# A hybrid convolution and attention layer on one core: column sums, weight norms and the first squares take another place in the order

## The chip, the cores and the metric

The kernel runs on one core of one Trainium2 chip. The metric is device time in microseconds (us) of one execution; the kernel before has a median of 2218.2 us over 3 runs (2217.41 to 2220.26). Its engines are TensorE (PE in the profile, its weight loads PEld), VectorE (DVE), ScalarE (ACT), GpSimd (POOL) and SyncE (SP), which here only starts DMAs.

## The reference

One layer on 4096 tokens of width 1024, in float32:

```
h = rmsnorm(x, norm_w)
u, g_b, g_c, z_conv, q, k, v, z_attn = split(h @ w_in, 8 pieces of 512 columns)
y_conv = g_b * (conv3(g_c * u, conv_w) + conv_b) * silu(z_conv)      # depthwise, width 3
q, k = rmsnorm(q, q_norm_w), rmsnorm(k, k_norm_w)                    # per head, 8 heads of 64
o = mix over (window, dilation) in ((128,1), (512,4), (2048,16)) of
    banded attention(q, k, v, T5 bias), weighted by a softmax over their log-sum-exps
y_attn = o * silu(z_attn)
out = x + concat(y_conv, y_attn) @ w_out
```

## The kernel before

Matmuls run in float16. Each operand is multiplied by a scale factor and split in a high and a low float16 part; a product is three matmuls, high·high, high·low and low·high (L401, L402, L403), summed in one PSUM bank. There are 8 banks of 128 x 512 float32.

**First phase** (to about 740 us of the trace). The tokens are cut into 32 tiles of 128. For each tile PE multiplies the tile by four groups of 512 columns of w_in: group 4 (q), 5 (k), 6 (v) and 7 (z, the attention's gate). One group of one tile is `mm`: 8 pieces of 128 along the depth, times 3, so 24 matmuls into one bank. Tile t uses the banks b0 to b0+3 with b0 = 4·(t mod 2), in the order q, k, v, z, so two tiles in a row fill the eight banks in turn. Tiles 0 and 1 are done together at the start, while the weights are still arriving: their q go to banks 0 and 1, k to 2 and 3, v to 4 and 5, z to 6 and 7.

What follows a group: `post_qk1` (ACT squares the bank, DVE L417 sums per head, DVE L237 and POOL L238 begin the inverse root by a power), `post_qk2` (DVE L244 to L247 finish it, DVE L425 reads the bank, ACT and DVE L433 split it, POOL L435 copies for k), `post_v` (DVE L448, ACT L450, DVE L451, store L452), `post_z` (ACT tanh L456, DVE L457, POOL L458, store L459). `x_split(t + 1)` makes the next tile ready: ACT L382 and DVE L383 write its high and low part, and two DMAs from SP's queue transpose them (L385). PE can start the next tile's q when both have landed. The input rows of tile t + 3 are asked of SP's queue by `load_x` (L204).

**v_sums, v_scales, v_gate.** The scale of v's columns comes from sums of absolute values of v's weights. PE adds them with 8 matmuls against ones (L475) into bank 1, DVE L476 reads the bank, L479 and L480 make the factor `vs` that `post_v` uses, L484 and L485 the factor that `post_z` uses. `post_v` and `post_z` of tiles 0 and 1 stand behind that.

**w_scale.** Each group of weights has one scale, from its norm. The weights come in 8 pieces of 128 x 512. ACT squares a piece and sums it (`w_square`), or DVE takes a maximum instead (`w_max`, L263). When all 8 are done, DVE L271 adds them, PE multiplies the 128 x 1 column by ones in bank 7 (L273, recorded as 2 instructions), DVE L274 reads it, POOL L276 takes a power, DVE L277 and on write the scales. `w_split` (ACT L295, DVE L296) then makes the two float16 parts of each piece. At the start this is done for group 4: four calls of `square` (each a `w_square` and a `w_max`), and among them `x_parts(1)`, which splits tile 1's transposed x from PSUM (ACT L375, DVE L376).

**conv_w_tasks.** The four convolution groups of w_in (order 0, 2, 3, 1) are scaled and split for the second phase by background tasks: for each group 8 loads with squares, then 8 loads with splits. From tile 4 on, `run_tasks` puts a batch of tasks behind `post_qk1` of k and another behind `post_z`, in each tile.

**What sets the order.** The schedule is written by hand: the order of the code is the order on each engine, each engine runs its own instructions strictly in that order, and waits between engines are semaphores. The pools of buffers (`wk`, `h16` with 3 buffers each, the staging buffers) give a new tile the buffer that comes free. `bias_copies` (L511) puts one DMA of 0.6 MB into ACT's queue in each of the tiles 10 to 17.

**Second phase.** Banded attention for three dilations, the convolution's matmuls (L838 to L840) and the output projection. Its first loads read the q and k that the first phase stored last.

Of the kernel before, what the change touches and what calls it, by code (L numbers as in the profile page):

```python
# [65 lines left out]
def tile_hybrid_block(  # L66
# [39 lines left out]
    def bank(n, shape, dt=F32):  # L106
        return ps.tile(shape, dt, name=f"bank{n % 8}")
# [57 lines left out]
    def run_tasks(tasks, n=None):  # L165
        for _ in range(len(tasks) if n is None else min(n, len(tasks))):
            tasks.pop(0)()
# [95 lines left out]
        nc.vector.tensor_reduce(wss[:, cg, kt:kt + 1], src, axis=AX.X, op=OP.max, apply_absolute_value=True)  # L263

    def w_scale(cg, maxima=0):
        if maxima:
            t = wss[:, cg, KT - maxima:]
            nc.vector.tensor_tensor(t, t, nwc[:, KT - maxima:], op=OP.mult)
            nc.vector.tensor_tensor(t, t, t, op=OP.mult)
        tot = pa.tile([128, 2], F32, name="wtot", bufs=2)  # L270
        nc.vector.tensor_reduce(tot[:, 0:1], wss[:, cg], axis=AX.X, op=OP.add)  # L271
        p = bank(7, [128, 512])
        nc.tensor.matmul(p[:, 0:1], ones, tot[:, 0:1], start=True, stop=True)  # L273
        nc.vector.tensor_scalar(tot[:, 1:2], p[:, 0:1], 1e-30, None, op0=OP.max)  # L274
        s = wsc[:, cg:cg + 1]
        nc.gpsimd.tensor_tensor(s, tot[:, 1:2], mhalf[:, 0:1], op=OP.pow)  # L276
        nc.vector.tensor_scalar(s, s, W_TOP, None, op0=OP.mult)  # L277
        nc.vector.tensor_scalar(nws[:, cg], nwc, s, None, op0=OP.mult)
        i = inv[:, cg:cg + 1]
        nc.vector.reciprocal(i, s)  # L280
        nc.vector.tensor_scalar(i, i, 1.0 / H_SCALE, None, op0=OP.mult)
        if cg in (4, 5):
            mul = 1.0 if cg == 4 else QK_SCALE
            c = rqs[:, cg - 4]
            nc.vector.tensor_scalar(c[:, 1:2], i, -0.5 * mul, None, op0=OP.mult)
            nc.vector.tensor_scalar(c[:, 2:3], i, 1.5 * mul, None, op0=OP.mult)
            nc.vector.tensor_scalar(c[:, 0:1], i, i, 1.0 / DH, op0=OP.mult, op1=OP.mult)
        if cg == 1:
            nc.vector.tensor_tensor(i, i, inv[:, 3:4], op=OP.mult)
        if cg in (3, 7):  # L290
            nc.vector.tensor_scalar(cz[:, cg // 4:cg // 4 + 1], i, 0.5, None, op0=OP.mult)
# [16 lines left out]
    wc = [[[None] * 4 for _ in range(4)] for _ in range(2)]  # L308

    def conv_w_tasks():  # L310
        tasks, got = [], {}
        todo = []
        for e, j in enumerate(CJ):
            todo += [(e, j, kt, 0) for kt in range(KT)] + [(e, j, kt, 1) for kt in range(KT)]

        def dma(n):
            e, j, kt, _ = todo[n]
            got[n] = stage_in(w_in_piece(j, kt))

        def use(n):  # L320
            e, j, kt, second = todo[n]
            src = got.pop(n)
            if not second:
                w_square(j, kt, src)
                if kt == KT - 1:
                    w_scale(j)
                return
            for sweep in range(2):
                if kt % 2 == 0:
                    wc[sweep][e][kt // 2] = wpool.tile([128, 2, 2, 256], F16, name=f"w{16 * sweep + 4 * e + kt // 2}")  # L330
                w = wc[sweep][e][kt // 2][:, kt % 2]
                w_split(w[:, 0], w[:, 1], src[:, 256 * sweep:256 * sweep + 256], j, kt)

        tasks += [lambda n=n: dma(n) for n in range(3)]
        for n in range(len(todo)):
            tasks.append(lambda n=n: use(n))
            if n + 3 < len(todo):
                tasks.append(lambda n=n: dma(n + 3))
        return tasks
# [31 lines left out]
    def x_parts(t, banks):  # L371
        hi, lo = h_views(t)
        for g, p in enumerate(banks):
            s = slice(4 * g, 4 * g + 4)
            nc.scalar.activation(hi[:, s], p, AF.Copy)  # L375
            nc.vector.tensor_tensor(lo[:, s], p, hi[:, s], op=OP.subtract)  # L376
# [17 lines left out]
    def mm(ts, j, cg, between=None, run=1):  # L394
        out = [bank(j + n, [128, 512]) for n in range(len(ts))]
        for k0 in range(0, KT, run):
            for n, (p, t) in enumerate(zip(out, ts)):
                hi, lo = HT[t]
                for kt in range(k0, k0 + run):
                    w = wa[(cg - 4) * 8 + kt]  # L400
                    nc.tensor.matmul(p, hi[:, kt, :], w[:, 0], start=kt == 0, stop=False)  # L401
                    nc.tensor.matmul(p, hi[:, kt, :], w[:, 1], start=False, stop=False)  # L402
                    nc.tensor.matmul(p, lo[:, kt, :], w[:, 0], start=False, stop=kt == KT - 1)  # L403
                    if n == len(ts) - 1:
                        for task in (between or {}).get(kt, ()):
                            task()
        return out
# [37 lines left out]
    def post_v(t, p):  # L445
        v16 = pa.tile([128, H, 128], F16, name="h16", bufs=3)
        v32 = pa.tile([128, 512], F32, name="wk", bufs=3)
        nc.vector.tensor_tensor(v32, p, vs, op=OP.mult)  # L448
        pv = v32.rearrange("p (h d) -> p h d", h=H)
        nc.scalar.activation(v16[:, :, 0:DH], pv, AF.Copy)  # L450
        nc.vector.tensor_tensor(v16[:, :, DH:128], pv, v16[:, :, 0:DH], op=OP.subtract)  # L451
        nc.sync.dma_start(v_d[t * 128:(t + 1) * 128], v16)  # L452

    def post_z(t, p):
        sz = pa.tile([128, 512], F32, name="wk", bufs=3)
        nc.scalar.activation(sz, p, AF.Tanh, scale=cz[:, 1:2])  # L456
        nc.vector.scalar_tensor_tensor(sz, sz, 1.0, p, op0=OP.add, op1=OP.mult)  # L457
        nc.gpsimd.tensor_tensor(sz, sz, vinv, op=OP.mult)  # L458
        nc.sync.dma_start(sz_d[t * 128:(t + 1) * 128], sz)  # L459
# [10 lines left out]
            nc.scalar.activation(VA[n], wa[16 + n][:, 0], AF.Abs)  # L470

    def v_sums():
        pcs = bank(1, [128, 512])
        for n in range(KT):
            nc.tensor.matmul(pcs, ones16, VA[n], start=n == 0, stop=n == KT - 1)  # L475
        nc.vector.tensor_scalar(vinv, pcs, 1e-30, None, op0=OP.max)  # L476

    def v_scales():
        nc.vector.reciprocal(vs, vinv)  # L479
        nc.vector.tensor_scalar(vs, vs, V_SCALE / H_SCALE, None, op0=OP.mult)  # L480

    def v_gate():

        nc.vector.tensor_scalar(vinv, vinv, inv[:, 6:7], inv[:, 7:8], op0=OP.mult, op1=OP.mult)  # L484
        nc.vector.tensor_scalar(vinv, vinv, 0.5 * H_SCALE / (V_SCALE * P_SCALE), None, op0=OP.mult)  # L485
# [54 lines left out]
    xp1 = x_transpose(1, 6)  # L540
    for n in range(4):
        square(4, n)
        if n == 1:
            x_parts(1, xp1)
    w_scale(4, 4)

    def each(f, *a):
        return lambda: f(*a)
# [1 line left out]
    def parts(cg):  # L550
# [10 lines left out]
    pv = mm((0, 1), 4, 6, {5: [each(w_scale, 7, 4)], 7: parts(7) + [  # L561
        each(stats1, 2), gains, each(post_qk1, 0, "q", pq[0]), each(stats2, 2)]})
# [8 lines left out]
    per = -(-len(tw) // (NT - 6))  # L571
    pq = mm((2,), 0, 4)[0]
    qk_store(1, "k")
    v_sums()
    v_scales()
    post_v(0, pv[0])
    post_v(1, pv[1])
    v_gate()
    post_z(0, pz[0])
    post_z(1, pz[1])  # L580
    for t in range(2, NT):
        b0 = 4 * (t % 2)
        post_qk1(t, "q", pq)
        if t + 3 < NT:
            load_x(t + 3)
        if t + 1 < NT:
            x_split(t + 1)
        post_qk2(t, "q")
        pk = mm((t,), b0 + 1, 5)[0]
        if 6 <= t < 9:  # L590
            bias_load(t - 6)
        post_qk1(t, "k", pk)
        if t + 2 < NT:
            stats1(t + 2)
        if t > 3:
            run_tasks(tw, per // 2)
        pv = mm((t,), b0 + 2, 6)[0]
        qk_store(t, "q")
        if t % 2 and t + 1 < NT:
            h_store(t // 2)  # L600
        post_qk2(t, "k")
        if t + 2 < NT:
            stats2(t + 2)
        post_v(t, pv)
        pz = mm((t,), b0 + 3, 7)[0]
        post_z(t, pz)
        if t > 3:
            run_tasks(tw, per - per // 2)
        if t + 1 < NT:
            pq = mm((t + 1,), 4 - b0, 4)[0]  # L610
        qk_store(t, "k")
        if 6 <= t < 9:
            bias_rows(t - 6)
        if 10 <= t < 10 + H:
            bias_copies(t - 10)
        if t == 12:
            taps()
        if t == 13:
            nc.vector.tensor_scalar(cw, cw, 0.5, None, op0=OP.mult)
        if t == NT - 3:  # L620
            load_h(0)
        if t == NT - 2:
            load_h(1)
# [319 lines left out]
    for gi, (pr, g, grp) in enumerate(groups):  # L943
        d = DILS[g]
        for b in range(8):
            if d == 16:
                n, nb = b % 2, 2
                vidx = (b // 2 + 4 * n, b // 2 + 4 * (1 - n))
            elif d == 4:
                n, nb, vidx = b, 8, (b, b + 1)  # L950
            else:
                n, nb, vidx = 8 * grp + b, 32, (b, b + 1)
# [191 lines left out]
    for u in range(NU):  # L1144
# [44 lines left out]
        n = u - LAG  # L1189
# [109 lines left out]
```

## Time and profile before

| what | value |
|---|---|
| median of 3 runs | 2218.2 us (2217.41 to 2220.26) |
| the profiled execution | 2221.63 us, span of the trace 2219.8 us |
| mean granted TensorE clock | 0.987 |
| PE busy | 2112.3 us, 95% of the span |
| DVE busy | 1440.1 us, 65% |
| ACT busy | 1071.0 us, 48% |
| POOL busy | 846.4 us, 38% |

The span is the trace's own time, from its first instruction to its last; the execution's time is 1.83 us longer. Times in the rows are counted from the start of the span. The granted clock is the share of its full speed that TensorE was allowed; it stands at 1.0 or at 0.5. A time in brackets behind a row is how long the engine had been idle before, and what released it.

### The profile page before, as it was taken

The numbers are of one execution on the slowest core, as the hardware profiler recorded it, in microseconds if no ns is written. First come the engines' busy times: TensorE is split into PE (matmuls) and PEld (weight loads), VectorE is DVE, ScalarE is ACT, GpSimd is POOL, SyncE is SP. The second block draws the span as 40 slices with busy tenths as digits, with TensorE's granted clock in tenths as the row PEclk, the third lists the DMA queues.
The fourth block names the chain that finished last, engine by engine and source line by source line (L and its number), as shares of the span: only waits on it lengthen the run. The fifth ranks groups of instructions, "written<-read, shape, count | busy, mean of one in ns | idle before, by whom it ended". The sixth has DMA issues, their size and how long they took to land. (4 is left out here: it accounts for less than half of the span.)

```text
span 2219.8 us, 48689 instructions
## 1 busy us (share of the span) xinstructions
PE 2112.3 (95%) x17718; PEld 1561.8 (70%) x17718; DVE 1440.1 (65%) x4031; ACT 1071.0 (48%) x3095; POOL 846.4 (38%) x1635
## 2 busy tenths in 40 slices
PE   7799999999999989999999999999999999999999
PEld 3344444444444778888888898888888887788887
DVE  6765655656565356766666666676666666887776
ACT  5433333333332156666666666676666664222221
POOL 0332322222322255433554335543353353344332
PEclk9999999999999999999999999999999999999999
DMA  5365567875654877779755896858966567687775
GB/s 200 95 176 154 153 173 163 205 162 156 169 165 134 180 157 144 149 160 179 154 140 129 175 195 135 175 139 173 189 135 151 123 121 221 208 266 243 240 247 184
DMA packets 627118, 378.36 MB, mean 170 GB/s; under 512 B 403393, under 2 KB 569404, under 8 KB 620732
## 3 DMA queue, kind: packets, MB, share of 16 engines
q1 hardware_dynamic: 505508, 304.71, 55.5%
q10 hardware_dynamic: 121368, 70.53, 12.4%
q8 instruction: 139, 2.28, 0.4%
q14 instruction: 103, 0.84, 0.1%
HBM read 174.54 MB, written 110.39 MB: 128 GB/s over the span
## 5 line engine op out<-in xcount | busy, mean ns | idle before, releaser
L838 PE MATMUL bank<-hb,w 128*128 128x256 f16 x2048 | 562.2, 275 | 0.3 <-ACT cu L845 0.3
L839 PE MATMUL bank<-hb,w 128*128 128x256 f16 x2048 | 562.2, 274 | 0.0
L840 PE MATMUL bank<-hb,w 128*128 128x256 f16 x2048 | 562.1, 274 | 0.0
L401 PE MATMUL bank<-wa,hb 128*128 128x512 f16 x1024 | 392.0, 383 | 17.0 <-DVE vinv L476 12.1
L403 PE MATMUL bank<-wa,hb 128*128 128x512 f16 x1024 | 391.5, 382 | 5.7 <-DMA hb<-xs 5.7
L402 PE MATMUL bank<-wa,hb 128*128 128x512 f16 x1024 | 391.8, 383 | 0.3 <-DVE wa L296 0.2
L1042 DVE CUSTOM_DVE_ANT_0 L<-bank,bt,alpha 128x256 f32<-128x256 f32 (+1 forms) x768 | 318.7, 452 | 111.9 <-PE bank L1030 81.6
L1051 ACT ACTIVATE L<-L,ot 128x256 f32<-128x256 f32 (+1 forms) x768 | 363.5, 476 | 27.9 <-DVE ot L1042 21.7
L1003 POOL COPY qz<-qk 64x128 f16<-64x128 f16 x512 | 156.4, 305 | 166.6 <-PE bank L1030 149.0
L840 PEld LDWEIGHTS <-w 128*128 128x128 f16 x2048 | 201.8, 99 | 24.6
L839 PEld LDWEIGHTS <-w 128*128 128x128 f16 x2048 | 201.8, 99 | 23.3 <-issue 0.5
L238 POOL TENSOR_TENSOR rs_rq<-rs_mq,mhalf 128x8 f32<-128x8 f32 x64 | 110.9, 1732 | 278.2 <-DVE rs_mq L237 275.8
L838 PEld LDWEIGHTS <-w 128*128 128x128 f16 x2048 | 201.9, 99 | 20.6
L1086 DVE SCALAR_TENSOR_TENSOR pt<-bank,pt 128x512 f16<-128x512 f32 x192 | 132.6, 690 | 119.0 <-ACT pt L1074 118.3
L1074 ACT ACTIVATE pt<-bank 128x512 f16<-128x512 f32 x192 | 114.6, 597 | 174.6 <-PE bank L1068 168.4
L402 PEld LDWEIGHTS <-hb 128*128 128x128 f16 x1024 | 100.9, 99 | 135.4 <-issue 18.1
L1105 PE MATMUL bank<-vt,pt 128*128 128x64 f16 x1536 | 176.6, 194 | 20.4 <-DMA pt<-src 16.5
L1090 DVE SCALAR_TENSOR_TENSOR src<-L,src 128x384 f16<-128x384 f32 (+1 forms) x192 | 131.6, 685 | 96.9 <-ACT src L1080 89.9
L403 PEld LDWEIGHTS <-hb 128*128 128x128 f16 x1024 | 100.9, 98 | 132.6 <-DMA hb<-xs 9.2
L401 PEld LDWEIGHTS <-hb 128*128 128x128 f16 x1024 | 101.7, 99 | 127.6 <-issue 6.2
L1107 PE MATMUL bank<-vt,pt 128*128 128x64 f16 x1536 | 176.9, 194 | 0.0
L1106 PE MATMUL bank<-vt,pt 128*128 128x64 f16 x1536 | 176.8, 194 | 0.0
(200 smaller groups left out, 4472.8 us busy)
## 6 DMA issues: line engine op xcount, KB each, us to landing
hb<-hT SPq DMA_DIRECT2D x32, 1024.0 KB, 6.9
o_d<-ot ACTq DMA_DIRECT2D x32, 528.0 KB, 5.1
qk<-o_d SPq DMA_DIRECT2D x63, 264.0 KB, 3.7
hT<-hb SPq DMA_DIRECT2D x16, 1024.0 KB, 4.1
wst<-in_w_in_dram SPq DMA_DIRECT2D x64, 256.0 KB, 2.9
qk<-in_x_dram SPq DMA_DIRECT2D x32, 512.0 KB
qk_d<-h SPq DMA_DIRECT2D x128, 96.0 KB, 3.4
vt<-v_d ACTq DMA_DIRECT2D x48, 256.0 KB, 4.5
```

The source lines that it names most:

```text
L401: nc.tensor.matmul(p, hi[:, kt, :], w[:, 0], start=kt == 0, stop=False)
L402: nc.tensor.matmul(p, hi[:, kt, :], w[:, 1], start=False, stop=False)
L403: nc.tensor.matmul(p, lo[:, kt, :], w[:, 0], start=False, stop=kt == KT - 1)
L838: nc.tensor.matmul(pt, w_h, hi[:, :, kt], start=kt == 0, stop=False)
L839: nc.tensor.matmul(pt, w_h, lo[:, :, kt], start=False, stop=False)
L840: nc.tensor.matmul(pt, w_l, hi[:, :, kt], start=False, stop=kt == KT - 1)
L1003: nc.gpsimd.tensor_copy(QZ[u % QZB][i][half], cols(q_t[i], U["qc"], half))
L1042: nc.vector.tensor_tensor_reduce(out=L[:, i], in0=p[i][:, 0:kn], in1=bias[:, U["b0"]:U["b0"] + kn], scale=alpha, scalar=BIG, op0=OP.add, o ...
L1051: nc.scalar.activation(L[:, i], L[:, i], AF.Exp, scale=-1.0, bias=ot[:, b, i, DH:DH + 1], accum_out=ot[:, b, i, DH + 1:DH + 2])
L1105: nc.tensor.matmul(p[:, i], hi, v[:, 0:DH], start=j == 0, stop=False)
L1106: nc.tensor.matmul(p[:, i], hi, v[:, DH:], start=False, stop=False)
L1107: nc.tensor.matmul(p[:, i], lo, v[:, 0:DH], start=False, stop=j == 1)
```

## The change

Three edits, all of the order of work; nothing is computed in another way.

First, `w_scale` becomes a generator `w_scale_steps` that pauses once, between DVE's sum (L271) and PE's matmul (L273). At the start all four `square` of group 4 are issued, then DVE's sum, then `x_parts(1)`, then the rest of the scale. Second, for the convolution's groups the part up to the pause stays where it was, behind the last square, and the rest is issued by the first task that splits a piece of that group. Third, `v_sums`, `v_scales`, `post_v` and `post_z` of tiles 0 and 1 are gathered in `late()`, which is called in tile 2 behind the k group's matmuls; the sums go to bank 3 instead of bank 1.

```diff
+    def w_scale_steps(cg, maxima=0):
         ...
         nc.vector.tensor_reduce(tot[:, 0:1], wss[:, cg], axis=AX.X, op=OP.add)
+        yield
         p = bank(7, [128, 512])
         nc.tensor.matmul(p[:, 0:1], ones, tot[:, 0:1], start=True, stop=True)
...
                 if kt == KT - 1:
-                    w_scale(j)
+                    scale.append(w_scale_steps(j))
+                    next(scale[0])
                 return
+            if kt == 0:
+                for _ in scale.pop():
+                    pass
             for sweep in range(2):
...
     def v_sums():
-        pcs = bank(1, [128, 512])
+        pcs = bank(3, [128, 512])
...
     for n in range(4):
         square(4, n)
-        if n == 1:
-            x_parts(1, xp1)
-    w_scale(4, 4)
+    scale = w_scale_steps(4, 4)
+    next(scale)
+    x_parts(1, xp1)
+    run_tasks([lambda: list(scale)])
...
     pq = mm((2,), 0, 4)[0]
     qk_store(1, "k")
-    v_sums()
-    v_scales()
-    post_v(0, pv[0])
-    post_v(1, pv[1])
-    v_gate()
-    post_z(0, pz[0])
-    post_z(1, pz[1])
+    def late():
+        v_sums()
+        ...
+        post_z(1, pz[1])
     for t in range(2, NT):
...
         pk = mm((t,), b0 + 1, 5)[0]
+        if t == 2:
+            late()
```

In the rows of the order, the line numbers of the changed kernel are 4 to 9 higher for the same instruction.

On VectorE at the start, before the first projection; `w_158` to `w_164` are the staged pieces of group 4, `hb_261` is the low part of tile 1's x. Before:

```order
L263 TENSOR_REDUCE wss<-w_158 128x1
L263 TENSOR_REDUCE wss<-w_160 128x1
L376 TENSOR_TENSOR hb_261<-bank_272,hb_261 128x512
L376 TENSOR_TENSOR hb_261<-bank_277,hb_261 128x512
L263 TENSOR_REDUCE wss<-w_162 128x1
L263 TENSOR_REDUCE wss<-w_164 128x1
L268 TENSOR_TENSOR wss<-wss,nwc 128x4
L269 TENSOR_TENSOR wss<-wss 128x4
L271 TENSOR_REDUCE wtot<-wss 128x1
L274 TENSOR_SCALAR wtot<-bank_302 128x1
```

and of the change:

```order
L263 TENSOR_REDUCE wss<-w_158 128x1
L263 TENSOR_REDUCE wss<-w_160 128x1
L263 TENSOR_REDUCE wss<-w_162 128x1
L263 TENSOR_REDUCE wss<-w_164 128x1
L272 TENSOR_TENSOR wss<-wss,nwc 128x4
L273 TENSOR_TENSOR wss<-wss 128x4
L275 TENSOR_REDUCE wtot<-wss 128x1
L385 TENSOR_TENSOR hb_261<-bank_272,hb_261 128x512
L385 TENSOR_TENSOR hb_261<-bank_277,hb_261 128x512
L279 TENSOR_SCALAR wtot<-bank_302 128x1
```

The two subtractions of `x_parts(1)` moved from among the four maxima to behind the sum.

On TensorE at the end of tile 2's q, the last two of the eight sums and what follows them; `wa_117` is the first piece of k's weights, `wa_125` of v's. Before:

```order
L475 LDWEIGHTS ones_220
L475 MATMUL bank_829<-w_696,ones_220 128x512
L475 LDWEIGHTS ones_220
L475 MATMUL bank_829<-w_698,ones_220 128x512
L401 LDWEIGHTS hb_646
L401 MATMUL bank_891<-wa_117,hb_646 128x512
```

and of the change:

```order
L484 LDWEIGHTS ones_220
L484 MATMUL bank_880<-w_696,ones_220 128x512
L484 LDWEIGHTS ones_220
L484 MATMUL bank_880<-w_698,ones_220 128x512
L410 LDWEIGHTS hb_646
L410 MATMUL bank_931<-wa_125,hb_646 128x512
```

The sums now stand behind tile 2's 24 matmuls of k and ahead of those of v, instead of ahead of k's.

On VectorE in the same place, behind the last instruction of tile 1's k (L433, L442 of the change). Before:

```order
L433 TENSOR_TENSOR h_795<-wk,h_795 128x4x128
L476 TENSOR_SCALAR vinv<-bank_829 128x512
L479 RECIPROCAL vs<-vinv 128x512
L480 TENSOR_SCALAR vs<-vs 128x512
L448 TENSOR_TENSOR wk<-bank_524,vs 128x512
L451 TENSOR_TENSOR h_841<-wk,h_841 128x8x64
L448 TENSOR_TENSOR wk<-bank_525,vs 128x512
L451 TENSOR_TENSOR h_847<-wk,h_847 128x8x64
L484 TENSOR_SCALAR vinv<-vinv,inv 128x512
L485 TENSOR_SCALAR vinv<-vinv 128x512
L457 SCALAR_TENSOR_TENSOR wk<-wk,bank_634 128x512
L457 SCALAR_TENSOR_TENSOR wk<-wk,bank_635 128x512
```

and of the change:

```order
L442 TENSOR_TENSOR h_795<-wk,h_795 128x4x128
L426 TENSOR_REDUCE ssq<-wk 128x8
L237 TENSOR_SCALAR rs_mq<-ssq,rqs 128x8
L392 SCALAR_TENSOR_TENSOR xs_839<-xt,rs_rx,xs_838 128x1024
L244 TENSOR_TENSOR rs_t_844<-rs_rq 128x8
L245 TENSOR_TENSOR rs_t_844<-rs_t_844,rs_mq 128x8
L246 TENSOR_SCALAR rs_t_844<-rs_t_844,rqs 128x8
L247 TENSOR_TENSOR rs_rq<-rs_rq,rs_t_844 128x8
L434 TENSOR_TENSOR wk<-bank_800,rs_rq 128x512
L437 TENSOR_TENSOR wk<-wk,cvec 128x512
L442 TENSOR_TENSOR h_852<-wk,h_852 128x4x128
L485 TENSOR_SCALAR vinv<-bank_880 128x512
```

The work of tile 2's q and the split of tile 3 went ahead of the eleven instructions on v and z of tiles 0 and 1; before, they stood right behind them.

## Rows read from the trace of the kernel before

**Rows 1.** The page, part 1: busy us (share of the span) x instructions.

```profile
PE 2112.3 (95%) x17718; PEld 1561.8 (70%) x17718; DVE 1440.1 (65%) x4031; ACT 1071.0 (48%) x3095; POOL 846.4 (38%) x1635
```

**Rows 2.** PE's waits, whole span: waited for; us, times, longest.

```profile
PE bank L1105 <- DMA pt<-src: 16.5, 6, 5.7
PE bank L273 <- DVE wtot L271: 13.2, 5, 3.9
PE bank L401 <- DVE vinv L476: 12.1, 1, 12.1
```

**Rows 3.** Timeline of PE, start: start us, us, engine line op.

```profile
20.79 0.58 PE L401 MATMUL bank<-wa,hb 128*128 128x512 f16 x1 [2.09 <-ACT wa L295]
```

**Rows 4.** Timeline of DVE, start.

```profile
12.69 1.27 DVE L263 TENSOR_REDUCE wss<-w 128x1 f32<-128x512 f32 x2
...
15.46 0.69 DVE L376 TENSOR_TENSOR hb<-bank,hb 128x512 f16<-128x512 f32 x1 [0.16 <-ACT hb L375]
16.07 1.27 DVE L263 TENSOR_REDUCE wss<-w 128x1 f32<-128x512 f32 x2
...
17.84 0.16 DVE L271 TENSOR_REDUCE wtot<-wss 128x1 f32<-128x8 f32 x1
18.74 0.16 DVE L274 TENSOR_SCALAR wtot<-bank 128x1 f32<-128x1 f32 x1 [0.74 <-PE bank L273]
```

**Rows 5.** Timeline of PE, tiles 2 to 4.

```profile
74.81 1.90 PE L475 MATMUL bank<-w,ones 128*128 128x512 f16 x8
88.76 0.59 PE L401 MATMUL bank<-wa,hb 128*128 128x512 f16 x1 [12.05 <-DVE vinv L476]
...
107.62 0.39 PE L403 MATMUL bank<-wa,hb 128*128 128x512 f16 x1 [0.22 <-DMA hb<-xs]
...
127.92 0.38 PE L401 MATMUL bank<-wa,hb 128*128 128x512 f16 x1
```

**Rows 6.** Timeline of DVE, tiles 2 and 3.

```profile
86.03 0.69 DVE L425 TENSOR_TENSOR wk<-bank,rs_rq 128x512 f32<-128x512 f32 x1
...
98.74 0.68 DVE L417 TENSOR_REDUCE ssq<-wk 128x8 f32<-128x512 f32 x1
...
99.59 2.30 DVE L383 SCALAR_TENSOR_TENSOR xs<-xt,rs_rx,xs 128x1024 f16<-128x1024 f32 x1
...
107.12 0.68 DVE L417 TENSOR_REDUCE ssq<-wk 128x8 f32<-128x512 f32 x1
...
117.81 1.27 DVE L383 SCALAR_TENSOR_TENSOR xs<-hb,rs_rx,xs 128x1024 f16<-128x1024 f32 x1
```

**Rows 7.** Timeline of POOL, tile 2.

```profile
98.31 2.51 POOL L458 TENSOR_TENSOR wk<-wk,vinv 128x512 f32<-128x512 f32 x2 [9.73 <-DVE wk L457]
```

**Rows 8.** Timeline of SP's queue, the transposes for tiles 3 and 4.

```profile
102.16 3.35 SPq L385 DMA_TRANSPOSE hb<-xs  x2
...
121.51 4.21 SPq L385 DMA_TRANSPOSE hb<-xs  x2
```

**Rows 9.** Timeline of PE, line 273, the convolution's second to fourth scale.

```profile
346.41 0.38 PE L273 MATMUL bank<-wtot,ones 128*128 128x1 f32 x2 [2.52 <-DVE wtot L271]
491.54 0.58 PE L273 MATMUL bank<-wtot,ones 128*128 128x1 f32 x2 [3.86 <-DVE wtot L271]
629.83 0.38 PE L273 MATMUL bank<-wtot,ones 128*128 128x1 f32 x2 [1.67 <-DVE wtot L271]
```

**Rows 10.** Windows of 5 us: PE, PEld, DVE, ACT, POOL busy, granted clock, DMA share, GB/s.

```profile
346.50:351.50 5.00, 5.00 (x17) 2.05 (x18) 0.93 (x6) 0.00 (x0) 0.80 (x2) 0.66 0.81 293
491.50:496.50 5.00, 4.96 (x17) 2.24 (x18) 2.42 (x12) 0.63 (x1) 1.80 (x4) 0.68 0.14 42
497.00:502.00 5.00, 5.00 (x25) 2.29 (x24) 2.42 (x7) 0.63 (x1) 0.55 (x1) 1.00 0.06 22
```

**Rows 11.** SP's queue near tile 15: timeline, then waits of 345 to 370 us.

```profile
356.65 10.80 SPq L385 DMA_TRANSPOSE hb<-xs  x2
...
SPq L385 <- DMA bv_d<-vec_d: 7.7, 1, 7.7
```

More of the change, by code (lines that the diff above doesn't have):

```diff
@@ L265, in w_scale @@
     def w_scale(cg, maxima=0):
+        for _ in w_scale_steps(cg, maxima):
+            pass
+    def w_scale_steps(cg, maxima=0):
         if maxima:
@@ L310, in conv_w_tasks @@
     def conv_w_tasks():
-        tasks, got = [], {}
+        tasks, got, scale = [], {}, []
         todo = []
@@ L325, in use @@
                 if kt == KT - 1:
-                    w_scale(j)
+                    scale.append(w_scale_steps(j))
+                    next(scale[0])
                 return
+            if kt == 0:
+                for _ in scale.pop():
+                    pass
             for sweep in range(2):
@@ L573, in tile_hybrid_block @@
     qk_store(1, "k")
-    v_sums()
-    v_scales()
-    post_v(0, pv[0])
-    post_v(1, pv[1])
-    v_gate()
-    post_z(0, pz[0])
-    post_z(1, pz[1])
+    def late():
+        v_sums()
+        v_scales()
+        post_v(0, pv[0])
+        post_v(1, pv[1])
+        v_gate()
+        post_z(0, pz[0])
+        post_z(1, pz[1])
     for t in range(2, NT):
```

## The prediction

> **What bounds the kernel now.** I read the page's part 1 first: PE is busy 95% of the span and no other engine over 65% [rows 1], so only time in which PE stands still, or runs at the lower clock, can be won. Next I read PE's waits [rows 2]. The change names three of them: 12.1 us before the first matmul of tile 2's k, once, until DVE L476 has read the column sums; 13.2 us in five waits for DVE's sum ahead of a scale (L273), of which three of the convolution's four are moved (2.52, 3.86 and 1.67 us) [rows 9]; and the start, where the first projection matmul comes at 20.79 us [rows 3]. Then I read the timelines of PE, DVE, POOL and SP around each place, to see what would hold PE back next. Two sizes serve everywhere. PE's step from matmul to matmul is (127.92 − 107.62) / 94 = 0.216 us [rows 5], so a group of 24 takes 5.2 us and a tile of 96 takes 20.7. And an idle stretch on PE is dear beyond its length: behind the wait of 3.86 us a window of 5 us holds 17 matmuls at a granted clock of 0.68, a later one 25 at 1.00 [rows 10], so the lower clock adds about 8 x 0.216 = 1.7 us. The waits of 12.05 and 3.86 us are followed at once by matmuls of 0.59 us instead of 0.38 [rows 5, 9]; the wait of 1.67 is not.
>
> **The start.** The scale of group 4 is a chain: four maxima on DVE, the sum L271, PE L273, DVE L274, POOL's power, the first split, PE's first L401 at 20.79 [rows 3, 4]. Between the second and third maximum stand tile 1's two L376 and a wait for ACT. In the new order the third maximum can start at 12.69 + 1.27 = 13.96 instead of 16.07, 2.1 us earlier, and the sum ends at 18.00 − 2.1 = 15.9. PE's matmul and its way back to L274 take 18.74 − 18.00 = 0.74, but the two L376 now lie in just that gap (0.69 and about 0.6): L274 waits for them, to about 17.2 instead of 18.74. I take −1.5 us; the bounds are −2.1 (if DVE's queue did not matter) and 0 (if the split waits for something else, such as the pieces' arrival).
>
> **Tile 2.** Before, PE ends the sums at 76.7 and stands idle until DVE L476 releases bank 1 at 88.76, because DVE works through q and k of tiles 0 and 1 first. Now PE goes on from 74.81 with tile 2's k, to 80.0. The sums follow, but in bank 3, which tile 1's k holds until DVE's L425 of 86.03 has ended at 86.72 [rows 6]: so 6.7 of the 12.05 us stay as idle time, only later. Sums at the lower clock to about 90.2, v to 95.4. Then z needs bank 3 too, and with it L476, which now stands behind tile 2's q and the split of tile 3 (about 8 us of DVE) and comes at about 95.5: no further wait to speak of. z and tile 3's q end at about 106.6, against 112.4 before: PE is up to 5.8 us ahead, and with 72 matmuls more would reach tile 4 at 122.1, where it stood there at 127.92.
>
> What is late next is tile 4's x. Its transposes leave SP at 121.51 to 125.72 behind L383 of 117.81 [rows 6, 8]; tile 3's left SP at 105.51 and were used by the first L403 that waited for them at 107.62 [rows 5, 8], 2.1 later, so tile 4's landed at about 127.8. That chain is DVE's, from 86.03 on, one instruction behind the other: the v and z work of tiles 0 and 1 (88 to 98.8), tile 2's q (L417 of 98.74), tile 3's split, tile 2's k (L417 of 107.12), tile 4's split (117.81). The change exchanges the first with the next two and leaves nothing out. Two of its members change: L383 of 99.59 took 2.30 us beside POOL's L458 against 1.27 for the other [rows 6, 7], which may now save 1.0; and k's power on POOL now queues behind the two L458 of 1.25 each [rows 7], which may cost 1.0. Queued behind it on DVE are k's remaining steps and L383 of tile 4, and behind that SP. So x lands at about 127.8 again, PE stands idle about 5 us before tile 4 and starts it at 127.5 (its high part needs only the first transpose), 0.4 us earlier, and behind a wait of that length comes the lower clock, +1.7. Before, the 12 us were followed by the same low stretch, which I have counted in the 90.2. I take **+1.3**. The bounds: −5.8 if DVE's chain holds PE nowhere, and +2.4 if the two z stores, which share the buffers of `wk`, also hold up tile 2's k.
>
> **The convolution's scales.** The first scale stays where it was, because its sum and its first split fall in the same batch: there the change does nothing. The second to fourth matmul moves two groups (48 matmuls, 10.4 us) later, long behind its sum, so the waits of 2.52, 3.86 and 1.67 us go [rows 9].
>
> - Second (346.41): 2.52 and a low stretch (17 matmuls, 0.66 [rows 10]), together 4.2 us at that place. But tile 15's x is late already: the second transpose stands in SP's queue for 7.7 us behind a copy of the biases and leaves only at 367.45 [rows 11], so it lands at about 369.5 by the 2.1 above. PE reached tile 15 at 346.66 + 96 x 0.216 + 1.7 + 0.4 (small waits) = 369.5 and did not wait. Four us earlier it waits four, and pays for the lower clock after it: 0 to +1.7, I take **+0.8** (bounds −4.3 and +1.7).
> - Third (491.54): 3.86 and its low stretch of 1.7. No copies of biases are left there and the transposes land well ahead: **−5.5** (−4.2 to −5.8).
> - Fourth (629.83): 1.67, no low clock behind it: **−1.8** (0 to −2).
>
> What hides the moved DVE and POOL work is that PE has 48 matmuls between; if that cover is gone (third rival) the splits come late.
>
> **Sum.** −1.5 + 1.3 + 0.8 − 5.5 − 1.8 = −6.7: from the profiled execution's 2221.6 (span 2219.8 and 1.8 around it) to 2214.9. That execution lies 3.4 above the median, so the forecast is 2218.2 − 6.7 = **2211.5 us**.
>
> **Rivals.** (1) *The transposes do not hold PE back.* At tile 15 alone the sum becomes −6.7 − 0.8 − 4.3 = −11.8, 2206.4; at tile 4 as well −11.8 − 1.3 − 5.8 = −18.9, 2199.3. For it: both landings are inferred from one tile's. Against it: the 7.7 us are a row of SP's own waits. The Trainium skill, "DMA: Bandwidth & Descriptors", section "Issuing engines are not separate DMA queues", says that DMAs started by different engines run on the same 16 DMA engines and interleave; by that rule a transpose would share the engines with the copy rather than stand behind it. The row shows it standing behind the copy, so the trace does not bear the rule out at this place. Chances 0.10 and 0.07.
>
> (2) *The gain is swallowed at the second phase.* PE there waits six times for DMAs of `pt`, 16.5 us in all, the longest 5.7 [rows 2]. If those transfers are bound by data that start with the phase and not with PE, up to 5.7 come back: 2217.2. Against it: their loads follow the last stores of the first phase, which move with PE. Chance 0.15.
>
> (3) *Slower.* The scale now stands right in front of its own splits. ACT's and DVE's splits wait for POOL's power, which can stand behind another power in the middle of a tile; the staging buffers come free later, SP's loads for them wait, and the next tile's transposes are behind those in SP's queue. It decides when the transposes of tiles 21 and 28 land more than 5.5 and 1.8 us behind where PE would then be. With each landing 3.3 us behind PE's arrival of before: −1.5 + 1.3 + 0.8 + 2 x 3.3 = +7.2, 2225.4. Against it: SP has no such wait elsewhere except behind the copies. Chance 0.05.
>
> **How the numbers follow.** The forecast has 0.60 and the rivals 0.10, 0.07, 0.15 and 0.05; 0.03 is left for low stretches that come or go elsewhere. A difference of 0.2%, 4.4 us, is about what a measurement of this kernel can tell from none. The forecast's own bounds are 2207 to 2215.5, since tile 4, tile 15 and the scales each carry about 1.7 us of clock. The range reaches over most of (1) and (2): 2204 to 2217.5. Faster: three quarters of the forecast, all of (1) and some of (2), 0.71. Same: the rest of both, 0.23. Slower: 0.06.
>
> **What would show it.** Right: the first L401 at about 19.3; PE's wait at the sums now for L425 and near 6.7 us; a wait of about 5 us for `hb` before tile 4 and of about 4 before tile 15; PE's waits for L271 down from 13.2 to about 5; tiles from 21 on 5 to 7 us earlier than before. Wrong: tile 4 starts near 122, or `hb` is waited for at tiles 21 and 28, or the last L403 of the first phase comes earlier and the end does not.

## The result, and the profile after

The changed kernel took 2205.0 us (median of 4 runs, 2200.2 to 2209.6), the kernel before beside it 2217.8: a ratio of 0.9943, 95% interval 0.9918 to 0.9969. Timed again beside the experiments it took 2208.7 (12 runs, 2203.8 to 2216.3) against 2216.5 (35 runs): 0.9970, 0.9954 to 0.9985. By these ratios the gain is 12.6 us in the first set and 6.6 in the second, which has three times the runs; the forecast was 6.7. The two intervals overlap between 7 and 10 us. The profiled execution took 2209.58 us with a span of 2207.8.

PE's busy time fell by 2.2 us and the span by 12.0: most of the gain is time in which PE stood idle.

```profile
PE 2110.1 (96%) x17718; PEld 1559.2 (71%) x17718; DVE 1436.5 (65%) x4031; ACT 1071.7 (49%) x3095; POOL 846.7 (38%) x1635
```

PE's waits over the whole span of the change (waited for: us in total, times, longest), against [rows 2]:

```profile
PE bank L1120 <- DMA pt<-src: 11.3, 5, 4.6
...
PE bank L410 <- DMA hb<-xs: 7.9, 4, 4.4
PE bank L484 <- DVE wk L434: 6.6, 1, 6.6
PE bank L412 <- DMA hb<-xs: 6.4, 8, 1.5
...
PE bank L278 <- DVE hb L385: 2.3, 1, 2.3
...
PE bank L410 <- ACT w L300: 2.0, 1, 2.0
PE bank L278 <- DVE wtot L275: 1.8, 1, 1.8
```

The 12.1 us for L476 are gone and 6.6 us for L434 (L425 before) stand in their place; of the 13.2 us for the scales' sums one wait of 1.8 is left, the first of the convolution's four, and group 4's 3.4 us have become 2.3 us for L385; the waits of the first matmul of a tile for its x (`hb`) have grown, 7.9 us where there had been 1.4. PE's timeline at the places that answer to [rows 3, 5] and to the second scale of [rows 9]:

```profile
17.10 0.59 PE L278 MATMUL bank<-wtot,ones 128*128 128x1 f32 x2 [2.26 <-DVE hb L385]
19.77 0.59 PE L410 MATMUL bank<-wa,hb 128*128 128x512 f16 x1 [2.08 <-ACT wa L300]
...
85.26 3.59 PE L484 MATMUL bank<-w,ones 128*128 128x512 f16 x8 [6.62 <-DVE wk L434]
...
125.05 0.61 PE L410 MATMUL bank<-wa,hb 128*128 128x512 f16 x1 [4.37 <-DMA hb<-xs]
...
344.37 0.39 PE L410 MATMUL bank<-wa,hb 128*128 128x512 f16 x1 [1.72 <-DMA hb<-xs]
...
390.38 0.39 PE L410 MATMUL bank<-wa,hb 128*128 128x512 f16 x1 [2.00 <-ACT w L300]
...
726.40 0.38 PE L412 MATMUL bank<-wa,hb 128*128 128x512 f16 x1
```

The bracket at 390.38 names ACT's split of a convolution weight, which this matmul does not read. With the scales alone (below) the same wait is put down to `hb`, and in both PE goes on 1.2 us after SP is done with tile 16's transposes, so I take it for a wait for `hb`.

The last row is the last matmul of the first phase. Before, it stood here, followed by the second phase's first:

```profile
733.46 0.38 PE L403 MATMUL bank<-wa,hb 128*128 128x512 f16 x1
733.67 0.27 PE L838 MATMUL bank<-hb,w 128*128 128x256 f16 x1
```

So the first phase gives 733.46 − 726.40 = 7.1 us, and the second phase of this one pair of traces 4.9 more. The same group in the two traces, at the groups where the distance changed, says where the 7.1 come from (us from the span's start; distance is after minus before):

| group | before | after | distance | what changed there |
|---|---|---|---|---|
| q of tiles 0, 1 | 20.79 | 19.77 | −1.0 | the start |
| q of tile 4 | 127.92 | 125.05 | −2.9 | ahead, less the wait of 4.37 |
| k of tile 4 | 133.10 | 133.10 | 0.0 | the lower clock behind that wait |
| k of tile 8 | 221.58 | 219.87 | −1.7 | a low stretch behind the first scale is gone |
| q of tile 14 | 346.66 | 344.37 | −2.3 | the second scale's 2.52, less 1.72 for `hb` |
| k of tile 16 | 396.14 | 396.85 | +0.7 | a wait of 2.0 and one of 1.1 |
| z of tile 20 | 498.50 | 493.25 | −5.3 | the third scale |
| q of tile 27 | 630.08 | 622.88 | −7.2 | the fourth scale |

### The profile page after: what moved, and what is told of

Read it like the earlier page. It is cut to its first block, busy times and chain, and to the rows that moved or that the text cites. A ratio compares the mean times of both kernels' runs of the same rounds, so it can differ in the third digit from the quotient of the medians.

```text
span 2207.8 us, 48685 instructions
## 1 busy us (share of the span) xinstructions
PE 2110.1 (96%) x17718; PEld 1559.2 (71%) x17718; DVE 1436.5 (65%) x4031; ACT 1071.7 (49%) x3095; POOL 846.7 (38%) x1635
## 5 line engine op out<-in xcount | busy, mean ns | idle before, releaser
L410 PE MATMUL bank<-wa,hb 128*128 128x512 f16 x1024 | 391.3, 382 | 12.1 <-DMA hb<-xs 7.9
L238 POOL TENSOR_TENSOR rs_rq<-rs_mq,mhalf 128x8 f32<-128x8 f32 x64 | 110.7, 1730 | 271.0 <-DVE rs_mq L237 264.0
```

## The experiments

Each is told by the last matmul of the first phase (733.46 before, 726.40 after), where the change acts, and by its time. A ratio is always against the kernel before in the same set of runs. Two profiles of the change end its first phase 1.0 us apart (726.40, and 725.37 in the table), and their tile 4's k comes 1.5 apart (133.10 and 131.57), so a difference of that size is not an edit's; "the change's" is the first of them.

**The change once more, and its three parts alone.** The edits are the three of the diff, each by itself.

> The changed kernel, timed once more beside the parts of the change. First theory (the prediction's, as the trace of the change has it): the first phase gives 7.1 us at its last matmul, and the 5 us beyond that come from the second phase, which happened to have fewer stretches at the lower clock and shorter waits for pt; then a second set of runs gives 2205 to 2212 us and the second phase's part changes from one profile to the next by some us while the first phase's 7.1 stays within 1. Rival: the second phase gains because it starts at another time against its transfers; then the 5 us come again: 2203 to 2207 us and the same places in the trace.

> Only the order at the start is changed (four squares, sum, then tile 1's split, then the rest of the scale). First theory: the first projection matmul comes 1.0 to 1.5 us earlier and k of tiles 0 and 1 1.5 us earlier, but tile 2 waits for DVE as before, so the gain is passed on only if DVE's queue is earlier too: 0 to -1.5 us, 2216 to 2218 us. Rival (any shift of the first phase changes the second by several us): 2212 or 2222 us with the first phase's end moved by less than 1.5.

> Only the sums of v's columns and the work on v and z of tiles 0 and 1 are moved. First theory: PE no longer waits 12 us before tile 2's k, waits 6.6 us before the sums and about 4.5 us before tile 4's first matmul, with a low stretch behind each: 0 to +1.5 us at tile 4's k, and the time +0 to +2, 2218 to 2220 us. Rival (tile 4 is held by something of the start, not by DVE's chain): tile 4 starts over 3 us earlier than before and the time falls to 2213 us.

> Only the scales of the convolution's weights are moved to their first split. First theory: nothing at tiles 14 to 17 (second transpose behind a copy of biases), -5.5 at tile 20 and -1.8 at tile 26, so the last matmul of the first phase comes 6 to 7.5 us earlier and the time is 2210 to 2212 us. Rival (the gain is given back where the second phase waits for transfers): first phase 6 to 7.5 earlier, time 2216 us or more.

| kernel | first phase ends | second phase, in the profile | median us | ratio, 95% interval |
|---|---|---|---|---|
| before | 733.46 | 1486.4 | 2216.5 (35 runs) | |
| the change again | 725.37 | 1480.6 | 2208.7 (12) | 0.9970, 0.9954 to 0.9985 |
| start alone | 733.10 | 1481.3 | 2215.4 (12) | 0.9998, 0.9981 to 1.0015 |
| column sums alone | 733.32 | 1491.4 | 2216.0 (12) | 1.0007, 0.9990 to 1.0024 |
| scales alone | 727.40 | 1479.9 | 2209.2 (12) | 0.9969, 0.9954 to 0.9983 |

The second phase's column is the span less the first. It runs over 11.5 us, and not with the first: the start alone and the column sums alone end their first phases 0.2 us apart and their second ones 10.1 apart. The 4.9 us that the first pair of traces shows there lie within this scatter; that no part of it is the change's I can't show from one profile each.

Against the kernel before of their own set, 1.7 us faster than the one that the expectations started from, the three times came as expected; that the scales would lose something at tiles 14 to 20 was not.

By the times the scales are the whole of the gain, as far as intervals of 3 to 4 us to either side can tell; by the first phase they are 6.1 of its 7.1 to 8.1 us. The column sums alone win their 12 us at tile 2 and hand them back at tile 4, where the row is

```profile
125.44 0.61 PE L401 MATMUL bank<-wa,hb 128*128 128x512 f16 x1 [4.51 <-DMA hb<-xs]
```

and the start alone is 1.1 us early at its first matmul and 0.4 at its last: on the way it loses 1.1 us at tile 20's z. The wait for the third scale is 3.86 us in both; the matmuls behind it, tile 20's v, take 7.6 us with a longer stretch at the lower clock, 6.5 in the trace of before and 5.2 at the full clock. With the column sums alone they take 7.5, so it is the trace of before that was lucky at this place.

**What holds tile 4: DVE's chain, tested by leaving one instruction out.** The factor of v is a constant here, so the output is not the layer's.

```diff
-        nc.vector.reciprocal(vs, vinv)
-        nc.vector.tensor_scalar(vs, vs, V_SCALE / H_SCALE, None, op0=OP.mult)
+        nc.vector.tensor_scalar(vs, vinv, 0.0, 1e-5 * V_SCALE / H_SCALE, op0=OP.mult, op1=OP.add)
```

> The change, but the reciprocal of v's column sums (DVE L488, 3.35 us) is left out and the factor is a constant, so what attention computes is not the layer's. First theory (DVE's chain holds tile 4's transposes): everything on DVE behind it is 3.3 us earlier, PE's wait for hb before tile 4's first matmul falls from 4.4 to about 1.2 us, and tile 4's k starts 3 to 4 us earlier than in the change (at 129 to 130 instead of 133.1, less what the start differs). Rival (SP's queue or the transposes themselves hold it): the wait stays over 3.5 us.

```profile
121.67 0.39 PE L410 MATMUL bank<-wa,hb 128*128 128x512 f16 x1 [1.19 <-DMA hb<-xs]
```

The wait fell from 4.37 to 1.19, by 3.18 us for 3.35 us of DVE, and the matmul behind it is at the full clock (0.39 instead of 0.61 us): tile 4's k came 5.8 us earlier, at 127.26 (4.3 against the change's second profile). The first phase ended at 719.58, and the one execution took 2201.7 us. DVE's chain holds the transposes, as the prediction had it.

**Filling DVE's waits for POOL.**

```diff
-        ... 1: [each(post_qk2, 0, "q"), each(post_qk1, 1, "q", pq[1])],
+        ... 1: [each(post_qk1, 1, "q", pq[1]), each(post_qk2, 0, "q")],
```

(and the same exchange at 3 and 5.)

> The change, and in tiles 0 and 1 the sum and power of the next group (post_qk1) stand ahead of the rest of the previous group (post_qk2), so that DVE need not stand still for POOL's power (waits of 1.76, 1.63 and 1.08 us before). First theory (DVE's chain from 62 us on sets both waits of tile 2 to 4): the wait at the sums falls from 6.6 us to 2 to 4 and the one before tile 4 from 4.4 to 0 to 2.5; at tile 4's k 2 to 6 us are won; at tiles 14 to 18 they are lost to the copies of biases; time -0 to -3 against the change, 2206 to 2209 us. Rival (these waits hang on ACT, POOL or SP): both waits stay within 1 us and the time too.

Measured: the wait at the sums 4.1 us (6.6 in the change's first profile, 5.2 in its second), the one before tile 4 still 4.4, tile 4's k 1.2 us earlier than in the change's first profile and 0.3 later than in its second, first phase's end 724.67, 2208.4 us (10 runs; ratio to before 0.9959, 0.9942 to 0.9977, not told apart from the change's). DVE's timeline tells why:

```profile
72.76 0.69 DVE L426 TENSOR_REDUCE ssq<-wk 128x8 f32<-128x512 f32 x1 [3.94 <-ACT wk L424]
```

The waits for POOL went and one of 3.94 us for ACT's square came. The expectation of 2 to 6 us was missed: a gap filled by order alone was replaced by another wait.

**Putting the split of tile 4 first.** Its statistics and its split stand in tile 2, ahead of the sums.

```diff
         pk = mm((t,), b0 + 1, 5)[0]
         if t == 2:
+            stats2(4)
+            x_split(4)
             late()
```

(with `stats1(4)` ahead of tile 3's split, and none of the three at its old place.)

> The change, and the statistics and the split of tile 4's x stand in tile 2, ahead of the sums of v's columns, instead of at the start of tile 3's round. First theory (tile 4's transposes end DVE's chain, so a split that is put ahead of the 10 us of work on v and z takes the wait away): no wait for hb before tile 4; about 2.5 us come back as a wait of tile 2's z for DVE's reading of the sums, which is that much later; tile 4's k starts 4 to 6 us earlier than in the change, and the low stretch behind the wait goes; first phase's end 3 to 6 us earlier, time 2203 to 2206 us. Rival (another wait takes its place in full: tile 3's q for the banks of v): tile 4's k within 1.5 us of the change's.

```profile
96.56 0.38 PE L410 MATMUL bank<-wa,hb 128*128 128x512 f16 x1 [2.79 <-DVE vinv L485]
...
122.45 0.38 PE L410 MATMUL bank<-wa,hb 128*128 128x512 f16 x1
```

No wait before tile 4, 2.79 us for DVE's reading of the sums instead, tile 4's k 5.5 us earlier (3.9 against the second profile), first phase's end at 719.08, 2204.2 us (6 runs, 0.9943, 0.9921 to 0.9965). The first theory holds, but for the first phase's end: 7.3 us earlier, 6.3 against the second profile, where 3 to 6 were expected. By the times alone this kernel can't be told from the change, whose two ratios are 0.9943 and 0.9970.

**Where the second scale's gain went: the copies of the biases.** First by moving them half a tile.

```diff
         post_qk2(t, "q")
+        if 10 <= t < 10 + H:
+            bias_copies(t - 10)
         pk = mm((t,), b0 + 1, 5)[0]
```

> The change, and each copy of the biases is issued from ACT's queue half a tile earlier in the code, behind the split of the next tile and tile t's q instead of behind the next tile's q matmuls, so that it starts just after a pair of transposes and not just before one. First theory (SP's second transpose stands behind the copy, and that takes what the scales win at tile 14): SP's waits of transposes for copies fall from 27.3 us to under 10, PE's waits for hb in tiles 12 to 19 (6 to 8 us with the low stretch) go, the first phase ends 3 to 5 us earlier, time 2204 to 2206 us. Rival (the transposes wait for the copy wherever it stands, because both share the DMA engines for 18 of 20.7 us): no gain, 2208 to 2210 us, with the waits in the same tiles.

SP's waits between 240 and 480 us, of the change and then of this kernel:

```profile
SPq L394 <- DMA bv_d<-vec_d: 27.3, 4, 7.1
SPq L204 <- DMA bv_d<-vec_d: 20.7, 3, 8.6
```

```profile
SPq L452 <- DMA bv_d<-vec_d: 44.2, 6, 11.2
SPq L461 <- DVE h L460: 14.9, 3, 7.2
SPq L394 <- DMA bv_d<-vec_d: 14.8, 1, 14.8
```

Why SP waits for a DMA of ACT's queue stands in the trace's records of the DMA issues, which carry the number of the semaphore that tells of a DMA's landing. Up to the end of the first phase the DMAs of both queues use eight numbers (101 to 103 and 105 to 109) in turn, and each waits, before it starts, until the DMA that had its number before has landed. In the change:

```profile
346.31 0.67 ACTq L520 DMA_DIRECT2D bv_d<-vec_d  x1
356.85 9.35 SPq L394 DMA_TRANSPOSE hb<-xs  x2
```

The copy has number 106, and so has the second of these transposes. SP stood before it from 358.13 until the copy landed at 364.90, and started it at 364.96; all that follows in SP's queue stood behind it. So a copy holds up not the DMA next to it but the one that has its number next.

The theory failed in its remedy: now the stores of q and k (L452) wait 44.2 us for the copies and one transpose 14.8, all in the one queue of SP. Half a tile earlier, the copies' numbers fall to other DMAs: six times to a store of q or k. The transpose that waited 14.8 us has the number of the copy of 335.72, and SP stood before it already when ACT issued that copy. PE waits 5.29 us before tile 17, the first phase ends at 735.01, 8.6 us later than the change's, and the time is 2218.6 us (12 runs; 1.0011, 0.9995 to 1.0027). Together with the exchange of `post_qk1` it was no better:

> Both of the two edits before, on top of the change. First theory: what is won at tile 4 is no longer lost at tiles 14 to 18, so the gains add: 5 to 10 us at the last matmul of the first phase and a time of 2200 to 2204 us, faster than the change. Rival (first phase's gains end at a fixed time of the transposes or of the second phase): no better than the better of the two.

2217.0 us (12 runs; 1.0004, 0.9986 to 1.0023), first phase's end 737.33.

Next the copies were cut in three, the same bytes in 24 DMAs instead of 8:

```diff
-        nc.scalar.dma_start(dap(bv_d, h * 3 * 128 * VEC, [[128 * VEC, 3], [VEC, 128], [1, VEC]]),
-                            dap(vec_d, h * 3 * VEC, [[VEC, 3], [0, 128], [1, VEC]]))
+        nc.scalar.dma_start(dap(bv_d, h * 128 * VEC, [[VEC, 128], [1, VEC]]),
+                            dap(vec_d, h * VEC, [[0, 128], [1, VEC]]))
...
-        if 10 <= t < 10 + H:
-            bias_copies(t - 10)
+        if t >= 8:
+            bias_copies(t - 8)
```

> The change, and each copy of the biases is cut in three that are issued one in each of the tiles 8 to 31 in place of one whole in each of the tiles 10 to 17. First theory (a transpose waits in SP's queue until the copy that was started before it has ended, so the copy's length sets the wait): the waits of SP's transposes for copies fall from 27 us to under 5, PE's waits for hb in tiles 12 to 19 go, the first phase ends 2 to 4 us earlier, time 2204 to 2207 us. Rival (the tiles 12 to 19 are late for the amount of data, or PE's waits there come from other places): the waits for hb stay or come at other tiles, time 2208 to 2212 us.

PE's waits from 60 to 740 us, the four longest of this kernel:

```profile
PE bank L484 <- DVE wk L434: 5.2, 1, 5.2
PE bank L410 <- DMA hb<-xs: 4.2, 1, 4.2
PE bank L278 <- DVE wtot L275: 1.8, 1, 1.8
PE bank L410 <- DVE wk L434: 1.5, 1, 1.5
```

SP waits for no copy any more between 240 and 480 us, PE from tile 3 on waits for `hb` only before tile 4, the first phase ends at 711.48, 14.9 us earlier than the change's, and the time is 2196.0 us (6 runs; 0.9907, 0.9885 to 0.9929). I had expected 2 to 4 us: I had counted the larger waits for `hb`, and not the low stretch nor the small waits of tiles 12 to 19; from tile 12's first matmul to tile 20's the two kernels part by 12.9 us. A piece lands 4.6 us after its start, and the DMA with its number starts mostly 7 to 10 us behind it and finds it free; a whole copy lands only after 12 to 19 us. So I take the length for what counts and not the spreading over more tiles, which the same edit does; no run has one without the other.

The same cut on the kernel before asks what the second scale's wait is worth where nothing behind it is late:

> The kernel before, without the change, with the copies of the biases cut in three and spread over the tiles 8 to 31. It asks what the change is worth where no transposes of tiles 14 to 18 are late. First theory (the second scale's 2.5 us and its low stretch were won by the change and lost again to the late transposes): with the copies cut, the wait for the scale ahead of tile 14 costs its full 4 us before, so the last matmul of the first phase comes 10 to 13 us later than in the change with cut copies (711.5), at 721 to 725, and the time is 2205 to 2209 us. Rival (the second scale's wait costs nothing for another reason, or the cut helps before more than after): 717 to 720, as far behind as the change is without the cut (7 us).

```profile
343.67 0.49 PE L273 MATMUL bank<-wtot,ones 128*128 128x1 f32 x2 [2.52 <-DVE wtot L271]
344.02 0.59 PE L401 MATMUL bank<-wa,hb 128*128 128x512 f16 x1
```

The first phase ends at 727.73, 16.3 us behind the change with cut copies; from the k of tile 13 to that of tile 14, across the second scale, 4.6 of them come (3.0 idle, 1.6 at the lower clock), and those are what the change lost to late transposes. The others are 1.0 at tile 4, 1.7 of a low stretch behind the first scale, 7.3 at the third scale, where the low stretch is 1.6 us dearer than in the trace of before, and 2.1 at the fourth, less 0.4 in small ones. The expected 10 to 13 us were exceeded; the rival's 717 to 720 is out. The time is 2208.0 us (12 runs; 0.9976, 0.9962 to 0.9990): on the kernel before the cut copies are worth 5.2 us, on the change 12.7.

**Both that helped.**

> Both edits on top of the change. First theory: the gains add, the first phase ends 6 to 9 us earlier than in the change, time 2199 to 2203 us, faster than the kernel before and the change. Rival (each gain is absorbed by the next wait): no better than the better of the two alone.

2191.0 us (6 runs, 2186.8 to 2195.0; 0.9885, 0.9864 to 0.9905), less than the 2199 to 2203 expected because the cut alone already was: faster than the kernel before by 25.7 us, and by 17.6 than the change as timed in another set of runs, in which the kernel before ran within 0.3 us of this set's. The first phase ends at 709.42, only 2.1 earlier than with the cut alone in this one profile: tile 4's k is 3.7 earlier (127.81 against 131.55), and 1.7 go to a low stretch at tile 8's q that the cut alone does not have. In the times the two gains add roughly (4.5 of 2208.7 − 2204.2, 12.7 of 2208.7 − 2196.0, 17.6 together).

## Why the prediction was right, step by step

**The start: −1.5 forecast, −1.0 to −1.2 measured** (first matmul at 19.77, 19.61 and, alone, 19.66; further on it can't be read, since k of tiles 0 and 1 comes 0.4 to 1.3 us earlier in kernels whose start is that of before). The maxima and the sum moved as worked out, 15.69 for the sum. The missing step is on PE: the two subtractions of `x_parts(1)` read the banks 6 and 7, and the scale's matmul writes bank 7. So L278 waits for the second of them ("2.26 <-DVE hb L385"), where I had let it run beside them. PE's row of before, which answers to the 17.10 above, and DVE's timeline after, against [rows 4]:

```profile
18.15 0.56 PE L273 MATMUL bank<-wtot,ones 128*128 128x1 f32 x2 [3.35 <-DVE wtot L271]
```

```profile
12.73 2.46 DVE L263 TENSOR_REDUCE wss<-w 128x1 f32<-128x512 f32 x4
...
15.69 0.16 DVE L275 TENSOR_REDUCE wtot<-wss 128x1 f32<-128x8 f32 x1
15.77 1.28 DVE L385 TENSOR_TENSOR hb<-bank,hb 128x512 f16<-128x512 f32 x2
17.72 0.16 DVE L279 TENSOR_SCALAR wtot<-bank 128x1 f32<-128x1 f32 x1 [0.68 <-PE bank L278]
```

**Tile 2 to 4: +1.3 forecast, +1.2 alone (from −1.3 at tiles 0 and 1 to −0.1 at tile 4's k), +1.5 and +1.1 in the change.** The wait at the sums (6.7 forecast, 6.6 measured, 5.2 in the second profile and alone), that of z (none forecast, at most 0.5), and the wait before tile 4 (5 forecast, 4.4 to 4.6) all stood where the trace of before put them. DVE's chain kept its length: the split of tile 4 ran at 116.35 instead of 117.81, 1.5 earlier as DVE was already at the L425 of tile 1's k (84.51 instead of 86.03). Both members that were to change did: tile 3's split took 1.28 us instead of 2.30, and L238 on POOL, behind the two L467, made DVE wait 1.1 us longer for the k of tile 2, before and after:

```profile
109.82 0.17 DVE L244 TENSOR_TENSOR rs_t<-rs_rq 128x8 f32<-128x8 f32 x1 [1.63 <-POOL rs_rq L238]
```

```profile
108.35 0.17 DVE L244 TENSOR_TENSOR rs_t<-rs_rq 128x8 f32<-128x8 f32 x1 [2.70 <-POOL rs_rq L238]
```

Mis-sized was the clock: behind the wait the window holds 12 matmuls where a full one holds 25 [rows 10], so 13 x 0.216 = 2.8 us and not 1.7. It hardly shows in the sum, because tile 4 started 1.3 us ahead of the start's gain instead of the forecast 0.4.

```profile
125.00:130.00 5.00, 4.95 (x12) 1.64 (x13) 3.56 (x11) 0.63 (x1) 2.12 (x3) 0.50 0.75 277
```

Not foreseen was that the low stretch behind the first scale (before, from 214.8 us) would be missing with this part, in all three profiles that hold it unaltered: −1.7. It is there in all four profiles without this part; of the ten with it, two have it (without the reciprocal, and with both edits that helped). Why is not shown.

**The second scale: +0.8 forecast, +1.7 with the scales alone, +1.8 and +2.4 in the change's two profiles** (from tile 13's z to tile 20's q). That the gain would be lost to transposes behind copies was right, and the cut copies show it: 4.6 us at that place once they are not late. The place was wrong. I had PE wait four us before tile 15; it waited 1.7 before tile 14, right where the scale's wait had been and with a low stretch behind it as before, and 2.0 before tile 16. The transposes of tile 14 were already late before (SP was done with them at 344.71, so they landed at about 345.9, when PE had stood since 343.9) and hidden under the scale's wait, and tile 15's moved with PE, since the copy ahead of them was issued at 346.31 instead of 347.98: I had taken that time as fixed.

**The third and fourth: −5.5 and −1.8 forecast, −5.8 and −2.1 measured**, in the change and with the scales alone alike. The third is measured against the short low stretch in the trace of before; against the three other profiles that have this wait it would be 0.9 to 1.5 us more.

**The sum is right in part by luck.** Of the first phase's 7.1 us in the first profile, the second scale took 1.0 us more than forecast and the start gave up to 0.5 less, and the low stretch behind the first scale, which no term had, gave 1.7. The waits that hold the sum, at the sums, before tile 4 and at the third and fourth scale, came as forecast.

**The rivals.** (1), that the transposes hold nothing back, is out by the waits themselves. The Trainium skill, "DMA: Bandwidth & Descriptors", section "Issuing engines are not separate DMA queues", has the DMAs of different engines interleave on the same 16 DMA engines. These rows neither bear that out nor speak against it, and the prediction read too much in them when it set them against the rule: in its 7.7 us the transpose had not been started. It waited in SP's queue for the copy's semaphore, and so did the others of the 27.3 us; with the copies cut in three none did. (2), a loss at the second phase, is out: with the scales alone the time falls by 7.3 us where the first phase falls by 6.1. (3), late splits, did not come: PE waits nowhere for `hb` at the tiles 21 and 28. The first timing of the change (12.6 us) was near twice the forecast; the second, with three times the runs, was not.

## What to carry to other kernels

A wait that is taken from the bounding engine is worth what the next thing behind it allows: look for work that is already late under its cover (here the transposes of tiles 4 and 14), and price it before counting the wait. Where DMAs of several queues take a few semaphores in turn, a long transfer holds up whichever DMA has its number next, in another queue too: cut the transfer before moving it. Moving it half a tile cost the first phase 8.6 us, cutting it in three (and spreading the pieces) won 14.9. Before a matmul is moved ahead of a reader, look up whose bank it writes.

## What the runs showed that I had not expected

The copies of the biases cost more than any wait of the change: 12.7 us of time on top of it, with no byte less. With the copies cut the change is worth about 15 us (ratios of 0.9907 and 0.9976, from two sets of runs), without that 6.6 to 12.6. And the second phase, whose instructions the change leaves in the same order, took from 1478.0 to 1491.4 us in the profiles of the kernels here, which differ only in the first phase, so a single pair of profiles of this kernel can't tell a difference of 5 us in the whole; the place where it arises can.
